# A streaming encoder layer: half sums and norm rows of the second token set inside the direct pairs, pooled products one group later

## The chip, the cores and the metric

The kernel runs on one core of a Trainium2 chip. The core's engines are TensorE (PE, with PEld for its weight loads), VectorE (DVE), ScalarE (ACT), GpSimd (POOL) and SyncE (SP), which issues the DMAs. The metric is the device time of one execution in microseconds, as a median of several; lower is better.

## The reference

One layer of a hybrid encoder works on 1024 prompt tokens and 64 sample tokens, 1088 in all, which share the weights. What is computed, cut to the core:

```python
h = rmsnorm(x); p = h @ w_in                      # split into qa, ka, va, qi, ki, wi, ub, qm, gates
a = sparse attention: per query, the top k keys by an indexer score are gathered
b = pool_mix(ub)                                  # see below
m = cross-attention of qm into 256 memory tokens
mixed = sum over the branches of sigmoid(gate) * (branch @ w_o)
x = x + mixed @ w_out
h = rmsnorm(x, g_ffn)
y = x + (silu(h @ w_gate) * (h @ w_up)) @ w_down  # D_FF = 2816

def pool_mix(u_ext):                              # 4 channel groups of 128, windows 2, 4, 8, 16
    mean_g = trailing mean of u over window_g
    p_g = mean_g - u_g
    return (p_g @ w_pool[g]) * s_pool
```

## The kernel before

All matrices are float32. Each operand is split into a rounded half `hi` and the rest `lo`, and a product is three matmuls (hi·hi, lo·hi, hi·lo). A weight block is loaded into a `raw` buffer by SP, rounded by ACT or POOL (`whi`), and its rest is taken by DVE (`wlo`, line 86).

The order of instructions on each engine is fixed when the kernel is built, by a scheduler that places them from a list of what depends on what, with gate products as fillers. An engine works through its list in order; a waiting instruction holds back all behind it.

**The pooled stage** (lines 388 to 448, in the trace from about 230 to 360 us). For each of four groups a `ub` block is multiplied (72 matmuls, into `e`), POOL doubles the window in `log2(window)` steps (`pw`, line 431), DVE forms the mean minus the token (line 435), ACT and DVE split it into `ph` and `pl` (lines 440 and 86), and three chunks of three matmuls with `pwh` and `pwl` make the pooled output, which ACT and DVE split into `bh` and `bl` (lines 446 and 447). At the same time DVE and ACT run the rounds that look for each query's k-th best score (`junk_v`, line 768; `junk_a`, line 765). PE has gate products (`fl`) as fillers, whose weights go through one buffer `fraw`. The next stage, `qm`, computes the queries of the memory attention, with weights `tmhi` and `tmlo`; the attention to memory follows at about 520 to 690 us.

**The feed-forward stage.** The tokens are two sets, 512 and 576. `w_gate` and `w_up` are walked in 11 pairs `p` of 128-row blocks. From pair 2 on, `hidden(p, (0, 1))` multiplies both sets through seven products on half sums instead of eight (`pair_product`, line 1115); seven sums of the inputs per k block (`block_sums`, lines 1061 to 1081) are needed for that. For the first set these sums are made early. For pairs 0 and 1 the first set is multiplied directly (`direct`, line 1144) while the norm rows (`norm_rows`: sums of squares line 1037, `rn` on DVE and POOL, `dg` line 1043, broadcast `ones` line 1055 into `rb`) and the sums of the second set are made; afterwards `hidden(p, (1,))` multiplies the second set for pairs 0 and 1. The sums use the tile `fr` (two buffers of 128x1024) and `ws` (four). In `pair_product` the `w_gate` blocks are loaded into `fr`, too, and the `w_up` blocks into `raw` (three buffers).

What the change touches in that stage, before:

```python
    EARLY = 2
    for p in range(EARLY):
        direct(p)
        if p == 0:
            rb = norm_rows(1, *st.pop())
        for k in (2 * p, 2 * p + 1):
            second_sums(k, rb)
```

Of the kernel before, what the change touches and what calls it, by code (L numbers as in the profile page):

```python
# [8 lines left out]
F32 = mybir.dt.float32  # L9
F32R = mybir.dt.float32r  # L10
AF = mybir.ActivationFunctionType
OP = mybir.AluOpType
# [33 lines left out]
def encoder_step(ctx: ExitStack, tc: tile.TileContext, a: dict, o: list):  # L46
# [38 lines left out]
    def lo_of(lo, src, hi):  # L85
        V.tensor_tensor(lo, src, hi.bitcast(F32), op=OP.subtract)  # L86
# [302 lines left out]
    if True:  # L389
        W0 = 15 + SEQ + 15  # L390
        E_ = W0 + DEC
        with tc.tile_pool(name="pool", bufs=1) as pp:
            fix = pp.tile([128, 4, 16], F32, name="fix")
# [9 lines left out]
            SP.dma_start(pwr.rearrange("p (g j) -> p g j", g=4), a["w_pool"])  # L403
            pwh = pp.tile([128, 4, 128], F32R, name="pwh")
            pwl = pp.tile([128, 4, 128], F32R, name="pwl")
            round_hi(pwh.rearrange("p g j -> p (g j)"), pwr)
            lo_of(pwl.rearrange("p g j -> p (g j)"), pwr, pwh.rearrange("p g j -> p (g j)"))
            for g, win in enumerate(WINDOWS):
                wts = [pp.tile([128, 1024], F32R, name=nm, tag=nm, bufs=1) for nm in ("uhi", "ulo")]
# [4 lines left out]
                for c0, cn in CH:  # L414
                    ps = mm()
                    gate_block((wh, wlo), hh[:, :, c0:c0 + cn], hl[:, :, c0:c0 + cn], ps[:, :cn])
                    m = min(cn, SEQ - c0)
                    A.copy(e[:, 15 + c0:15 + c0 + m], ps[:, :m])
                    if m < cn:
                        A.copy(e[:, W0:E_], ps[:, m:cn])  # L420
                ps = mm()
                PE.transpose(ps[:15, 0:128], e[:, SEQ:SEQ + 15], ident)
# [12 lines left out]
                V.scalar_tensor_tensor(cur[:, 31:], cur[:, 31:], 1.0 / win, e[:, 31:], op0=OP.mult, op1=OP.subtract)  # L435
                ph = pp.tile([128, T], F32R, name="ph", tag="ph", bufs=1)
                pl = pp.tile([128, T], F32R, name="pl", tag="pl", bufs=1)
                for d0, d1, s0 in ((0, SEQ, 15), (SEQ, T, W0)):
                    src = cur[:, s0:s0 + d1 - d0]
                    A.copy(ph[:, d0:d1], src)  # L440
                    lo_of(pl[:, d0:d1], src, ph[:, d0:d1])
                for c0, cn in CH:
                    c1 = c0 + cn
                    ps = mm()[:, :cn]
                    matmul3(ps, [(pwh[:, g], pwl[:, g], ph[:, c0:c1], pl[:, c0:c1])])
                    A.activation(bh[:, g, c0:c1], ps, AF.Copy, scale=spool_c[:, g:g + 1])
                    V.scalar_tensor_tensor(bl[:, g, c0:c1], ps, spool_c[:, g:g + 1], bh[:, g, c0:c1].bitcast(F32),
                                           op0=OP.mult, op1=OP.subtract)

    with tc.tile_pool(name="qm", bufs=1) as tp:  # L450
        for half in range(2):
            w = tm_weights(tp, a["w_qm"][half], 256)
            for b in range(NB):
                t0, n = TS[b]
                ps = token_major(w, b, 256)
                qn = tp.tile([128, 2, 128], F32, name="qn", tag="qn", bufs=2)
                head_norm(tp, ps, n, 2, 128, qn[:n])
                SP.dma_start(q_m[t0:t0 + n, half * 256:(half + 1) * 256], qn[:n].rearrange("p h d -> p (h d)"))


# [626 lines left out]
    def pair_product(name, p, sets, outs, finish):  # L1087
        raws = []
        for e in range(2):
            raw = fa.tile([128, 1024], F32, name="fr", tag="fr", bufs=2) if name == "w_gate" else raw_tile()  # L1090
            SP.dma_start(raw.rearrange("p (k j) -> p k j", k=KT), a[name][p + e * NP])
            raws.append(raw)
# [50 lines left out]

    def direct(p):
        n = SETS[0][1]
# [3 lines left out]
        for name in ("w_gate", "w_up"):  # L1149
            for e in range(2):  # L1150
                w = wblock(a[name][p + e * NP], (KT, 128))
                for c in range(2):
                    ps = mm()[:, :h]
                    matmul3(ps, [(w[0][:, k], w[1][:, k], blocks[c][k // 4][0][:, k % 4], blocks[c][k // 4][1][:, k % 4])
                                 for k in range(KT)])
                    t = g[:, e, c * h:c * h + h]
                    if name == "w_gate":
                        A.activation(t, ps, AF.Silu)
                    else:
                        V.tensor_tensor(t, ps, t, op=OP.mult)  # L1160
                if name == "w_up":
                    SP.dma_start(u_d[p][e, :, :n], g[:, e])

    def hidden(p, sets):
# [23 lines left out]
        pair_product("w_up", p, sets, v, up_last)  # L1188

    turn2, pair_w = [0], []  # L1190
    u_d = [dram.tile([2, 128, T], F32, name=f"u{p}") for p in range(NP)]
# [30 lines left out]

    EARLY = 2
    for p in range(EARLY):
        direct(p)
        if p == 0:
            rb = norm_rows(1, *st.pop())
        for k in (2 * p, 2 * p + 1):
            second_sums(k, rb)
    fu_c.__exit__(None, None, None)  # L1230
# [105 lines left out]
```

## Time and profile before

| | |
|---|---|
| median of three runs | 1779.03 us (1777.31 to 1780.24) |
| the profiled execution | 1782.27 us |
| its span | 1780.5 us |
| mean granted PE clock | 0.991 |
| PE busy | 1721.8 us (97%), 11810 instructions |
| DVE busy | 1127.0 us (63%) |
| ACT busy | 816.4 us (46%) |
| POOL busy | 403.3 us (23%) |
| pair products (line 1115), their share of the chain that ended last | 24% |

The profile is of one execution, a few microseconds longer than the median; the 1.8 us between span and execution lie outside what the trace records. "Busy" counts an engine's instructions; a share over the whole span is a mean over stages with different limits, so the stages that the change touches are read by themselves. A timeline row reads: start us, duration us, engine, line, operation, output <- inputs, shapes, count, and in brackets how long the engine was idle before it and what released it.

### The profile page before, as it was taken

To read this page: it belongs to the slowest core of one execution; us is meant where nothing else is said; L and a number is where in the kernel's file an instruction comes from. 1 tells how busy PE (TensorE), PEld (TensorE's weight loads), DVE (VectorE), ACT (ScalarE), POOL (GpSimd) and SP (SyncE) were. 2 spreads that over 40 slices of the span, in tenths; PEclk is the share of its full clock that TensorE was granted. 3 is DMA by queue.
4 is the path that set the end of the run, shared out by engine and by line. 5 is a ranking of instruction groups with operands and counts; after the bars stand their busy time and mean duration, and the time that the engine had idled before them with its cause. 6 is when DMAs were issued, how large, how long until landed. Compare 5 with 4: busy or idle time off the path is not lost.

```text
span 1780.5 us, 31511 instructions
## 1 busy us (share of the span) xinstructions
PE 1721.8 (97%) x11810; PEld 1672.4 (94%) x11810; DVE 1127.0 (63%) x2411; ACT 816.4 (46%) x1927; POOL 403.3 (23%) x444
## 2 busy tenths in 40 slices
PE   7999999999999998989899998999999999999999
PEld 6999999989999998877798997999999999999999
DVE  6567999998953345779783858645444444544443
ACT  5456677726523443579631444433333333433332
POOL 4111423343531223765203521100000000000000
PEclk9999999999999999999999998999999999999999
DMA  7122541134355236640454333222222221857562
GB/s 230 60 67 76 164 141 57 58 98 137 118 157 176 84 97 233 188 154 1 165 184 146 98 120 110 92 73 73 73 73 77 92 75 38 316 184 239 187 229 98
DMA packets 128582, 224.26 MB, mean 126 GB/s; under 512 B 23463, under 2 KB 86303, under 8 KB 128430
## 3 DMA queue, kind: packets, MB, share of 16 engines
q1 hardware_dynamic: 128430, 222.26, 38.5%
q8 instruction: 93, 1.52, 0.3%
q14 instruction: 59, 0.48, 0.1%
HBM read 167.84 MB, written 54.37 MB: 125 GB/s over the span
## 4 chain that ended last, share of the span: by engine, by line
PE 61%; DVE 6%; DMA 2%; issue 1%; POOL 1%; ACT 1%; SPq 0%; DVEq 0%; ACTq 0%; POOLq 0%
PE mm L1115 24%; PE mm L1263 14%; PE mm L120 11%; PE fl L120 7%; PE acc L921 1%; PE tr L891 1%; DVE lo L86 1%; PE mm L914 1%; DVE wlo L86 1%; DVE fr L1071 1%; DMA side_a<-gt 1%; DVE ws L1078 0%; PE mm L603 0%; DVE pr L895 0%; DVE pl L86 0%
## 5 line engine op out<-in xcount | busy, mean ns | idle before, releaser
L1115 PE MATMUL mm<-hi,whi 128*128 128x288 f32 (+1 forms) x1120 | 324.0, 289 | 9.4 <-ACT whi L1107 8.3
L1115 PE MATMUL mm<-hi,wlo 128*128 128x288 f32 (+1 forms) x1120 | 324.9, 291 | 0.0
L1115 PE MATMUL mm<-lo,whi 128*128 128x288 f32 (+1 forms) x1120 | 324.2, 290 | 0.0
L1115 PEld LDWEIGHTS mm<-hi,whi 128*128 128x128 f32 x1120 | 212.6, 190 | 10.1 <-ACT whi L1107 8.5
L1115 PEld LDWEIGHTS mm<-lo,whi 128*128 128x128 f32 x1120 | 212.5, 190 | 0.0
L1115 PEld LDWEIGHTS mm<-hi,wlo 128*128 128x128 f32 x1120 | 211.9, 189 | 0.2 <-DVE wlo L86 0.2
L120 PE MATMUL fl<-hl,whi 128*128 128x362 f32 (+1 forms) x576 | 190.5, 331 | 0.0
L120 PE MATMUL fl<-hh,whi 128*128 128x362 f32 (+1 forms) x576 | 189.9, 330 | 0.6 <-ACT hh L133 0.6
L120 PE MATMUL fl<-hh,wlo 128*128 128x362 f32 (+1 forms) x576 | 189.3, 329 | 0.0
L1263 PE MATMUL mm<-uh,wh 128*128 128x362 f32 (+1 forms) x512 | 167.4, 328 | 0.0
L1263 PE MATMUL mm<-ul,wh 128*128 128x362 f32 (+1 forms) x512 | 166.8, 326 | 0.0
L1263 PE MATMUL mm<-uh,wl 128*128 128x362 f32 (+1 forms) x512 | 166.0, 326 | 0.0
L86 DVE TENSOR_TENSOR wl<-raw,wh 128x1024 fp32r<-128x1024 f32 x64 | 78.4, 1225 | 126.1 <-ACT wh L94 125.8
L94 ACT CAST wh<-raw 128x1024 fp32r<-128x1024 f32 x64 | 67.3, 1051 | 148.9 <-PE mm L1263 137.5
L120 PE MATMUL mm<-tmhi,hh 128*128 128x256 f32 (+3 forms) x432 | 122.8, 289 | 0.5 <-POOL tmhi L96 0.5
L120 PE MATMUL mm<-tmlo,hh 128*128 128x256 f32 (+3 forms) x432 | 122.5, 286 | 0.3 <-DVE tmlo L86 0.3
L120 PE MATMUL mm<-tmhi,hl 128*128 128x256 f32 (+3 forms) x432 | 122.3, 285 | 0.0
L765 ACT ACTIVATE junk_a<-score,cand_a,sgn_a 128x512 f16<-128x512 f32 (+2 forms) x93 | 95.5, 1027 | 46.8 <-DVE cand_a L782 22.7
L86 DVE TENSOR_TENSOR wlo<-raw,whi 128x1024 fp32r<-128x1024 f32 (+1 forms) x75 | 76.1, 1027 | 55.0 <-ACT whi L1107 39.7
L120 PEld LDWEIGHTS fl<-hh,whi 128*128 128x128 f32 x576 | 108.3, 188 | 1.6 <-issue 1.0
L120 PEld LDWEIGHTS fl<-hl,whi 128*128 128x128 f32 x576 | 108.4, 188 | 0.6
L120 PEld LDWEIGHTS fl<-hh,wlo 128*128 128x128 f32 x576 | 108.5, 188 | 0.6
(386 smaller groups left out, 4538.5 us busy)
## 6 DMA issues: line engine op xcount, KB each, us to landing
raw<-in_w_down_dram SPq DMA_DIRECT2D x66, 512.0 KB, 3.7
raw<-in_w_up_dram SPq DMA_DIRECT2D x26, 512.0 KB, 3.7
fraw<-in_w_gates_dram SPq DMA_DIRECT2D x24, 512.0 KB, 4.0
fr<-in_w_gate_dram SPq DMA_DIRECT2D x22, 512.0 KB, 3.6
side<-side_a SPq DMA_DIRECT2D x8, 1088.0 KB, 6.0
raw<-in_w_out_dram SPq DMA_DIRECT2D x16, 512.0 KB, 3.7
uf<-u SPq DMA_DIRECT2D x44, 181.0 KB, 3.7
u<-tg SPq DMA_DIRECT2D x22, 288.0 KB, 2.1
```

What stands on the lines that cost most here:

```text
L86: V.tensor_tensor(lo, src, hi.bitcast(F32), op=OP.subtract)
L94: A.copy(hi, src)
L120: PE.matmul(ps, l, r, start=i == 0, stop=i == n - 1)
L765: A.activation(junk[:n, :nk], sc, AF.Sign, bias=bj, scale=1.0 if scale is None else scale[:n, j:j + 1], accum_out=sj)
L891: PE.matmul(lg[:n, i * 512:i * 512 + cn], qT[:, h, :n], kT[:, kv, s, k0 + c:k0 + c + cn], start=s == 0, stop=s == 1)
L914: PE.transpose(pt[:cn, i * n:(i + 1) * n], probs[i][:, c:c + cn], ident[:n, :n])
L921: PE.matmul(acc, vv, r, start=ji == 0 and i == 0, stop=ji == nj - 1 and i == 1)
L1071: V.scalar_tensor_tensor(hb[e][:, :n], ys[i][:, kk], gffn_c[:, kk:kk + 1], rb[:, :n], op0=OP.mult, op1=OP.mult)
L1115: PE.matmul(dst[i], l, r, start=start and j == 0, stop=stop and j == 11, skip_group_check=True)
L1263: PE.matmul(acc[f], l, r, start=kb == 0 and j == 0, stop=kb == NF - 1 and j == 2)
```

## The change

- In the pooled stage, the three chunks of products of a group (now `pooled`) are issued after the `ub` block of the next group; those of the last group in the `qm` stage, ahead of its fifth token block. `ph`, `pl`, `pwh` and `pwl` lie in a pool of their own (`phl`), which lives until the end of `qm`.
- `direct` takes a table `between` of what to do ahead of a weight block. The second set's norm rows are issued ahead of the second `w_gate` block of pair 0, its sums ahead of the two `w_up` blocks of pair 0 and the two `w_gate` blocks of pair 1.
- In `pair_product` the `w_gate` blocks of pairs 0 and 1 go to `raw` and their `w_up` blocks to `fr`; from pair 2 on it is as before.

```diff
--- before.py
+++ after.py
@@ -389,6 +389,10 @@
     if True:
         W0 = 15 + SEQ + 15
         E_ = W0 + DEC
+        phl_c = tc.tile_pool(name="phl", bufs=1)
+        phl = phl_c.__enter__()
+        pwh = phl.tile([128, 4, 128], F32R, name="pwh")
+        pwl = phl.tile([128, 4, 128], F32R, name="pwl")
         with tc.tile_pool(name="pool", bufs=1) as pp:
             fix = pp.tile([128, 4, 16], F32, name="fix")
             SP.dma_start(fix, bass.AP(tensor=a["fix"].tensor, offset=a["fix"].offset, ap=[[0, 128], [16, 4], [1, 16]]))
@@ -401,10 +405,18 @@
             A.copy(hc, ps[:, :64].rearrange("p (g t) -> p g t", g=4)[:, :, :15])
             pwr = raw_tile()[:, :512]
             SP.dma_start(pwr.rearrange("p (g j) -> p g j", g=4), a["w_pool"])
-            pwh = pp.tile([128, 4, 128], F32R, name="pwh")
-            pwl = pp.tile([128, 4, 128], F32R, name="pwl")
             round_hi(pwh.rearrange("p g j -> p (g j)"), pwr)
             lo_of(pwl.rearrange("p g j -> p (g j)"), pwr, pwh.rearrange("p g j -> p (g j)"))
+            def pooled(g, ph, pl):
+                for c0, cn in CH:
+                    c1 = c0 + cn
+                    ps = mm()[:, :cn]
+                    matmul3(ps, [(pwh[:, g], pwl[:, g], ph[:, c0:c1], pl[:, c0:c1])])
+                    A.activation(bh[:, g, c0:c1], ps, AF.Copy, scale=spool_c[:, g:g + 1])
+                    V.scalar_tensor_tensor(bl[:, g, c0:c1], ps, spool_c[:, g:g + 1], bh[:, g, c0:c1].bitcast(F32),
+                                           op0=OP.mult, op1=OP.subtract)
+
+            wait = []
             for g, win in enumerate(WINDOWS):
                 wts = [pp.tile([128, 1024], F32R, name=nm, tag=nm, bufs=1) for nm in ("uhi", "ulo")]
                 wh, wlo = wblock(a["w_ub"][g], (KT, 128), None, wts)
@@ -418,6 +430,8 @@
                     A.copy(e[:, 15 + c0:15 + c0 + m], ps[:, :m])
                     if m < cn:
                         A.copy(e[:, W0:E_], ps[:, m:cn])
+                if wait:
+                    pooled(*wait.pop())
                 ps = mm()
                 PE.transpose(ps[:15, 0:128], e[:, SEQ:SEQ + 15], ident)
                 PE.transpose(ps[:15, 128:256], e[:, E_ - 15:E_], ident)
@@ -433,29 +447,27 @@
                 V.tensor_tensor(cur[:, 15:31], cur[:, 15:31], fix[:, g], op=OP.mult)
                 V.tensor_tensor(cur[:, 15:31], cur[:, 15:31], e[:, 15:31], op=OP.subtract)
                 V.scalar_tensor_tensor(cur[:, 31:], cur[:, 31:], 1.0 / win, e[:, 31:], op0=OP.mult, op1=OP.subtract)
-                ph = pp.tile([128, T], F32R, name="ph", tag="ph", bufs=1)
-                pl = pp.tile([128, T], F32R, name="pl", tag="pl", bufs=1)
+                ph = phl.tile([128, T], F32R, name="ph", tag="ph", bufs=1)
+                pl = phl.tile([128, T], F32R, name="pl", tag="pl", bufs=1)
                 for d0, d1, s0 in ((0, SEQ, 15), (SEQ, T, W0)):
                     src = cur[:, s0:s0 + d1 - d0]
                     A.copy(ph[:, d0:d1], src)
                     lo_of(pl[:, d0:d1], src, ph[:, d0:d1])
-                for c0, cn in CH:
-                    c1 = c0 + cn
-                    ps = mm()[:, :cn]
-                    matmul3(ps, [(pwh[:, g], pwl[:, g], ph[:, c0:c1], pl[:, c0:c1])])
-                    A.activation(bh[:, g, c0:c1], ps, AF.Copy, scale=spool_c[:, g:g + 1])
-                    V.scalar_tensor_tensor(bl[:, g, c0:c1], ps, spool_c[:, g:g + 1], bh[:, g, c0:c1].bitcast(F32),
-                                           op0=OP.mult, op1=OP.subtract)
+                wait.append((g, ph, pl))
 
     with tc.tile_pool(name="qm", bufs=1) as tp:
         for half in range(2):
             w = tm_weights(tp, a["w_qm"][half], 256)
             for b in range(NB):
+                if half == 0 and b == 4:
+                    pooled(*wait.pop())
                 t0, n = TS[b]
                 ps = token_major(w, b, 256)
                 qn = tp.tile([128, 2, 128], F32, name="qn", tag="qn", bufs=2)
                 head_norm(tp, ps, n, 2, 128, qn[:n])
                 SP.dma_start(q_m[t0:t0 + n, half * 256:(half + 1) * 256], qn[:n].rearrange("p h d -> p (h d)"))
+
+    phl_c.__exit__(None, None, None)
 
 
     with tc.tile_pool(name="qa", bufs=1) as qp:
@@ -1087,7 +1099,7 @@
     def pair_product(name, p, sets, outs, finish):
         raws = []
         for e in range(2):
-            raw = fa.tile([128, 1024], F32, name="fr", tag="fr", bufs=2) if name == "w_gate" else raw_tile()
+            raw = raw_tile() if (name == "w_up") == (p >= EARLY) else fa.tile([128, 1024], F32, name="fr", tag="fr", bufs=2)
             SP.dma_start(raw.rearrange("p (k j) -> p k j", k=KT), a[name][p + e * NP])
             raws.append(raw)
         a11, a12 = raws[0][:, :512], raws[0][:, 512:]
@@ -1141,13 +1153,15 @@
         product(chain, a22, 3, False, True, lambda i: finish(i, t21[i], chain[i]))
 
 
-    def direct(p):
+    def direct(p, between={}):
         n = SETS[0][1]
         h = n // 2
         blocks = [[(HH[0][0][q], HH[0][1][q]) if q is not None else b12_hl for q in qs] for qs in ((0, 1), (None, 2))]
         g = fu.tile([128, 2, n], F32, name="tg", tag="tg", bufs=2)
         for name in ("w_gate", "w_up"):
             for e in range(2):
+                if (name, e) in between:
+                    between[name, e]()
                 w = wblock(a[name][p + e * NP], (KT, 128))
                 for c in range(2):
                     ps = mm()[:, :h]
@@ -1187,6 +1201,7 @@
 
         pair_product("w_up", p, sets, v, up_last)
 
+    EARLY = 2
     turn2, pair_w = [0], []
     u_d = [dram.tile([2, 128, T], F32, name=f"u{p}") for p in range(NP)]
     sq0 = out_proj(0)
@@ -1220,13 +1235,10 @@
     def second_sums(k, rb):
         block_sums(1, k, rb, HH[1], [fa.tile([128, 512], F32, name="ws", tag="ws", bufs=4) for e in range(4)])
 
-    EARLY = 2
-    for p in range(EARLY):
-        direct(p)
-        if p == 0:
-            rb = norm_rows(1, *st.pop())
-        for k in (2 * p, 2 * p + 1):
-            second_sums(k, rb)
+    rbs = []
+    direct(0, {("w_gate", 1): lambda: rbs.append(norm_rows(1, *st.pop())),
+               ("w_up", 0): lambda: second_sums(0, rbs[0]), ("w_up", 1): lambda: second_sums(1, rbs[0])})
+    direct(1, {("w_gate", 0): lambda: second_sums(2, rbs[0]), ("w_gate", 1): lambda: second_sums(3, rbs[0])})
     fu_c.__exit__(None, None, None)
     yp_c.__exit__(None, None, None)
     dn_c = tc.tile_pool(name="dn", bufs=1, side="right")
```

DVE in the first direct pair, before, from the second set's norm factors on (`rn`, `dg`; `wlo` are rests of weights of `direct`, `tg` its gated outputs, `fr<-y` the first step of a sum):

```order
L1039 TENSOR_SCALAR rn<-mm 128x5
L1043 TENSOR_SCALAR dg<-ident,rn 128x128 x5
L86 TENSOR_TENSOR wlo<-raw,whi 128x1024 x2
L1160 TENSOR_TENSOR tg<-mm,tg 128x256 x2
L86 TENSOR_TENSOR wlo<-raw,whi 128x1024
L1160 TENSOR_TENSOR tg<-mm,tg 128x256 x2
L86 TENSOR_TENSOR wlo<-raw,whi 128x1024
L1071 SCALAR_TENSOR_TENSOR fr<-y_10642,gffn_c,rb 128x576 x2
L1078 TENSOR_TENSOR ws<-fr 128x288
```

The same place after:

```order
L1051 TENSOR_SCALAR rn<-mm 128x5
L1055 TENSOR_SCALAR dg<-ident,rn 128x128 x5
L86 TENSOR_TENSOR wlo<-raw,whi 128x1024
L1083 SCALAR_TENSOR_TENSOR fr<-y_10646,gffn_c,rb 128x576 x2
L1090 TENSOR_TENSOR ws<-fr 128x288
L86 TENSOR_TENSOR lo_12280<-fr,hi_12273 128x288
L1090 TENSOR_TENSOR ws<-fr,ws 128x288
L86 TENSOR_TENSOR lo_12282<-fr,hi_12275 128x288
L86 TENSOR_TENSOR lo_12281<-fr,hi_12274 128x288
```

Before, four direct weight blocks and four outputs stood between `dg` and the first sum; now one weight block does, and sums and weight blocks alternate.

SP's queue before, from the last output of the first direct pair (`u` written from `tg`; `raw<-in_w_up` is the first pair's `w_up` for the products on half sums, `uf` a load for the last stage):

```order
L1162 DMA u_11269<-tg 128x512
L1091 DMA raw<-in_w_up_dram 128x1024 x3
L1162 DMA u_11270<-tg 128x512
L1254 DMA uf<-u_11269 128x364 x2
L1162 DMA u_11270<-tg 128x512
L1091 DMA fr<-in_w_gate_dram 128x1024 x4
L1091 DMA raw<-in_w_up_dram 128x1024 x2
L1183 DMA u_11269<-tg_12878 128x576
```

and after:

```order
L1176 DMA u_11273<-tg 128x512
L1103 DMA raw<-in_w_gate_dram 128x1024
L1266 DMA uf<-u_11273 128x364 x2
L1103 DMA fr<-in_w_up_dram 128x1024
L1103 DMA raw<-in_w_gate_dram 128x1024
L1103 DMA fr<-in_w_up_dram 128x1024
L1103 DMA raw<-in_w_gate_dram 128x1024
L1176 DMA u_11274<-tg 128x512 x2
L1103 DMA raw<-in_w_gate_dram 128x1024
```

The first two pairs' `w_gate` loads stood behind the last output of the direct stage, in `fr`; now three of them and two `w_up` loads go out ahead of these outputs, `w_gate` into `raw` and `w_up` into `fr`.

PE at the first group's pooled products (`mm<-ph,pwh`), before; `fl` is a filler, `uhi` the weights of the next `ub` block:

```order
L120 MATMUL fl<-hh,whi 128x362
L120 MATMUL fl<-hl,whi 128x362
L120 MATMUL fl<-hh,wlo 128x362
L120 MATMUL mm<-ph,pwh 128x364
L120 MATMUL mm<-ph,pwh 128x362 x2
L120 MATMUL mm<-hh,uhi 128x364
L120 MATMUL mm<-hl,uhi 128x364
L120 MATMUL mm<-hh,ulo 128x364
```

and after:

```order
L120 MATMUL mm<-hl,uhi 128x362
L120 MATMUL mm<-hh,ulo 128x362
L120 MATMUL mm<-hh,uhi 128x362
L120 MATMUL mm<-hl,uhi 128x362
L120 MATMUL mm<-hh,ulo 128x362
L120 MATMUL mm<-ph,pwh 128x364
L120 MATMUL mm<-pl,pwh 128x364
L120 MATMUL mm<-ph,pwl 128x364
L120 MATMUL mm<-ph,pwh 128x362
```

The pooled products stood behind fillers and ahead of the next `ub` block; now they stand behind that block. Between the first and the last pair of transposes of `e` (line 422 before, 436 after) PE has 506 rows before, of which 257 are fillers, and 316 after, of which 67 are fillers; DVE has 17 rounds on 64x192 before, 10 after.

## Rows read from the trace of the kernel before

**Rows 1.** Waits of PE, 1000 to 1140 us: total us, times, longest.

```profile
PE mm L1115 <- ACT whi L1107: 8.3, 1, 8.3
```

**Rows 2.** Windows: us; PE, PEld, DVE, ACT, POOL busy; PEclk; DMA share; GB/s.

```profile
1030.00:1055.00 25.00, 25.00 (x212) 25.00 (x212) 7.74 (x15) 7.10 (x11) 2.56 (x2) 1.00 0.37 116
1055.00:1077.80 22.80, 22.70 (x190) 22.50 (x188) 21.63 (x45) 12.13 (x31) 6.46 (x3) 1.00 0.28 92
1077.80:1086.00 8.20, 0.01 (x1) 0.01 (x1) 5.50 (x14) 3.59 (x9) 0.85 (x1) 0.63 0.64 205
1086.00:1109.50 23.50, 23.02 (x156) 22.56 (x156) 18.99 (x30) 11.54 (x24) 5.09 (x3) 0.91 0.28 85
```

**Rows 3.** Timeline of DVE, second half sums: start, us, operation.

```profile
1055.69 1.54 DVE L1071 SCALAR_TENSOR_TENSOR fr<-y,gffn_c,rb 128x576 f32<-128x576 f32 x2
...
1082.83 0.44 DVE L86 TENSOR_TENSOR lo<-ws,hi 128x288 fp32r<-128x288 f32 x1
```

**Rows 4.** Chain of waits, 1060 to 1140 us: start, us, what.

```profile
1079.98 5.24 DMA fr<-in_w_gate_dram
...
1085.99 23.04 PE mm L1115 x156
...
1109.57 22.62 PE mm L1115 x168
```

**Rows 5.** Waits of PE, 242 to 520 us.

```profile
PE fl L120 <- DVE fpt L549: 3.1, 2, 1.8
PE mm L120 <- ACT ph L440: 2.9, 2, 1.8
PE mm L120 <- DVE pl L86: 1.6, 1, 1.6
```

**Rows 6.** Windows, 242 to 500 us.

```profile
242.00:500.00 258.00, 251.30 (x1719) 247.76 (x1718) 239.40 (x687) 153.18 (x458) 99.55 (x108) 0.98 0.29 91
```

**Rows 7.** Timelines of PE and DVE around the second norm rows.

```profile
1034.01 0.72 PE L1037 MATMUL mm<-ones,sq 128*128 128x1 f32 x6
1034.60 0.36 PE L120 MATMUL mm<-hi,whi 128*128 128x256 f32 x1
...
1036.23 1.07 DVE L1043 TENSOR_SCALAR dg<-ident,rn 128x128 f32<-128x128 f32 x5 [1.29 <-POOL rn L1040]
1037.27 1.23 DVE L86 TENSOR_TENSOR wlo<-raw,whi 128x1024 fp32r<-128x1024 f32 x1
...
1053.39 1.22 PE L1055 MATMUL mm<-dg,ones 128*128 128x128 f32 x10
```

**Rows 8.** Timelines of DVE and ACT before the second pair ends.

```profile
1127.94 1.29 DVE L86 TENSOR_TENSOR wlo<-raw,whi 128x512 fp32r<-128x512 f32 x2 [1.25 <-ACT whi L1107]
...
1132.09 0.62 ACT L1107 CAST whi<-fr 128x512 fp32r<-128x512 f32 x1 [3.36 <-PE mm L1115]
```

**Rows 9.** Tile `fr`, 1070 to 1180 us, its loads.

```profile
DMA to landing us min/median/max: 3.6/3.7/5.2
```

**Rows 10.** Lines 435 and 422: duration ns least/median/most, first and last start.

```profile
L435 DVE SCALAR_TENSOR_TENSOR pw<-pw,e x4: 1283/1284/1285, 256.0 to 352.8; 128x1087 f32<-128x1087 f32 x4
...
L422 PE MATMUL mm<-ident,e x4: 270/272/275, 252.7 to 338.9; 128*15 128x128 f32 x4
```

**Rows 11.** Timelines of DVE and POOL, 235 to 252 us.

```profile
235.63 1.21 DVE L86 TENSOR_TENSOR ulo<-raw,uhi 128x1024 fp32r<-128x1024 f32 x1
...
242.90 0.41 DVE L768 TENSOR_SCALAR_CACHE_REDUCE junk_v<-score,cand_v 64x192 f16<-64x192 f32 x1
...
247.18 0.40 DVE L768 TENSOR_SCALAR_CACHE_REDUCE junk_v<-score,cand_v 64x192 f16<-64x192 f32 x1
...
251.66 2.84 DVE L86 TENSOR_TENSOR ulo<-raw,uhi 128x1024 fp32r<-128x1024 f32 x1
...
251.36 2.05 POOL L431 TENSOR_TENSOR pw<-e 128x1117 f32<-128x1117 f32 x1 [1.39 <-ACT e L420]
```

**Rows 12.** Timeline of PE, end of memory attention.

```profile
688.20 0.44 PE L120 MATMUL fl<-bh,whi 128*128 128x384 f32 x1 [1.40 <-DVE bl L86]
```

## The prediction

> **What bounds the kernel now.** I read four views in turn: the waits of TensorE (PE), the busy time by stretch, the chain of waits around the longest stall, and the timelines of the engines that PE waits for. PE is busy 97% of the span, so a change of order gains only where PE waits, or where it runs at the lower clock for having waited. Near the change the list of waits has one large entry: the pair products of the feed-forward part (L1115) wait once, 8.3 us, for a rounded weight, `whi` [rows 1]. By stretch [rows 2], this is the join between the two direct pairs and the first pair on half sums: PE is full until 1077.8 (22.70 of 22.80 us), does nothing until 1086, and runs at a granted clock of 0.91 in the pair after that. VectorE (DVE) shows why. It is busy 7.74 of 25 us in the first direct pair and 21.63 of 22.80 us in the second, because all of the second set's half sums are computed there: the first starts at 1055.69 and the last ends at 1083.27 [rows 3]. These sums use the two `fr` buffers, which the first `w_gate` blocks need too. So the chain [rows 4] runs through the sums to the load of `fr`, issued at 1079.98 and landed 5.24 later; behind a cast PE starts at 1085.99.
>
> The other place is the pooled stage (242 to 520 us): PE waits 3.1 for `fpt`, 2.9 for `ph` and 1.6 for `pl` there [rows 5], at a mean clock of 0.98 over 258 us with DVE busy 239 of 258 us [rows 6]. PE is kept full by gate fills (`fl`) between the pooled products.
>
> **The change part by part.** The sum is made against the profiled execution, 1782.27 us, which lies 3.24 above the median of 1779.03.
>
> *1. Sums inside the direct pairs, first gate weights through `raw`.* In the new order the sums start behind the `dg` rows of the first pair instead of at 1055.69, 18 us earlier by the trace (`dg` ends at 1037.30 [rows 7]). DVE has 25 − 7.74 = 17.3 us free in the first pair's stretch [rows 2]. The sums of the old second stretch spill 1083.27 − 1077.8 = 5.5 us past it; the room is three times that, so they end about 10 us before the direct pairs do. The first `w_gate` block now takes a `raw` buffer that the direct weights leave, and is issued before the last direct products. The wait disappears: **−8.3**. What is late next is the second `w_gate` block. SP issues it behind two `uf` loads and one `fr` load; the first product on a sum needs it one product after the first, 23.04/7 = 3.3 us later [rows 4]. I see it land 3 to 5 us ahead.
>
> *2. The clock behind the stall.* The first pair on half sums was busy 23.04 us where the next was 22.62 [rows 4]: **−0.4**. The clock of 0.91 over 23.5 us would allow 2.1 [rows 2]; since the pair's own length shows 0.4, I take that, and 2.1 as the bound.
>
> *3. Norm rows inside the first pair.* Before, 19 us lay between the sums of squares (1034.01) and the broadcast through `dg` (1053.39) [rows 7], so nothing waited. In the new order PE has 12 products in between. At 22.70/190 = 0.12 us each [rows 2] they end at 1034.60 + 1.44 = 1036.04, while DVE's last `dg` ends at 1036.23 + 1.07 = 1037.30 behind a power on GpSimd (POOL). PE waits **+1.3**. Everything on PE is queued behind it. Bounds: 0, if the sums of squares finish earlier because two of the five are now done ahead, and 2.6 if the weight block in front of `dg` on DVE delays it by its own duration (1.23 [rows 7]).
>
> *4. Pair 1 to pair 2.* `w_up` of pair 1 now sits in `fr`, and `w_gate` of pair 2 wants the same two buffers, where `raw` and `fr` alternated before. The last reader of the first block's second half is a split that ends, as the first of two, at 1127.94 + 0.65 = 1128.59 [rows 8]. A load to `fr` lands 3.6, 3.7 or 5.2 us after issue (least, median, most) [rows 9], the cast takes 0.62: PE could start at 1128.59 + 3.7 + 0.62 = 1132.91. Before, the cast stood at 1132.09, so PE started at 1132.71. **+0.3** with hops of 0.1; bounds 0.1 and 1.8 (landing 5.2). The landing decides. The Trainium skill ("DMA: Bandwidth & Descriptors", "Issuing engines are not separate DMA queues") says that all transfers interleave on the same 16 engines, and this load now meets stores of `u` and loads of `w_up`; by it the 5.2 would be the one to take and the sum would be 1.5 worse. The rows show the median nearer to the least, with the same neighbours, so I keep 0.3.
>
> *5. Pooled products one group later.* Nothing is computed that was not before; the pooled products, 9 per group, move behind the next group's `ub` block, and the last into the `qm` stage. Their waits for `ph` and `pl`, 4.5 us [rows 5], lose their direct cause, since a whole `ub` block of PE work now lies between. But the scheduler also draws the four groups together. PE's transposes ran from 252.7 to 338.9 and DVE's pooled combination from 256.0 to 352.8 [rows 10]: 86.2 and 96.8 us. Counted in the two orders, PE has 506 rows between first and last transpose before and 316 now, of which fills 257 and 67; at 86.2/506 = 0.170 each that is 53.8 us. DVE loses 7 selection rounds of 4.28 us (242.90 to 247.18) and 3 splits of 1.21 [rows 11], which makes 96.8 − 30.0 − 3.6 = 63.2. DVE falls behind PE by 10.6 before and by 9.4 now. Before, 257 fills stood there to cover it; now 67, worth 67 × 0.170 = 11.4 us, just enough. Gain of waits and loss of cover are of one size, so **0**. Bounds: −12.8 (all of [rows 5]'s 7.6 and the clock's 0.02 × 258 = 5.2 [rows 6]) and +14.3 (below, third rival).
>
> *6. Fills kept for later.* About 160 gate fills now stand at the end of memory attention, where 11 stood, and the last values finish earlier. PE's wait of 1.40 for `bl` at 688.20 [rows 12] should go: **−1.0**, bounds −1.4 and 0, as its filler could be late itself.
>
> Sum: −8.3 − 0.4 + 1.3 + 0.3 + 0 − 1.0 = −8.1, so 1774.2 in a profiled execution and **1771** as a median.
>
> **The rivals.**
>
> *The pooled stage gains too.* The waits of 4.5 us lose their cause and those for `fpt` could go with them; against it, DVE stays as busy as it was. With half to all of the 12.8: 1758 to 1765 (−8.1 − 6.4 and −8.1 − 12.8 from 1779).
>
> *The direct wait comes back in part.* For it: SP issues in order, and the second `w_gate` block stands behind `uf` and `fr` loads. If it is issued no earlier than the old first one (1079.98) it lands at the same 1085.22, and PE, which has one product of 3.3 us to do, waits 5.0: the sum is −3.1, with part 4 at its bound −1.6, so 1776 to 1777.5. Against it: its buffer is free once the direct weights are split, some microseconds earlier.
>
> *DVE sets the pooled stage, and it is slower than before.* A split next to a pooling step on POOL (2.05 us at 251.36) took 2.84 instead of 1.21 us [rows 11], 1.63 more. There are 1 + 2 + 3 + 4 = 10 such steps, and they now lie closer together. If each meets one DVE instruction of that kind, DVE is 16.3 later; of 9.4 + 16.3 = 25.7 the fills cover 11.4, so PE waits up to 14.3. With −8.1 that is 1785 as a median; with half the meetings, 1777. It decides once DVE's lateness passes the 11.4 us of fills by more than the 8.1 gained elsewhere, 19.5. For it: DVE busy 93% [rows 6] and a quarter of the fills. Against it: before, the steps met such instructions as well, so part of the 16.3 is in the 96.8 already. The Trainium skill ("SBUF — State Buffer", "Who interferes with whom") states that a DVE instruction with two SBUF inputs and a POOL instruction that reads SBUF shut each other out for a whole instruction. The split of 2.84 agrees; by the rule each meeting could cost up to the 2.05 of the step, 20.5 in all, and the time would be 1789.
>
> *Less than it says.* Should the scheduler's new order leave the sums where DVE is late anyhow, 1779 would stand; the order shows them moved, so I give this no share of its own.
>
> **How the numbers follow.** A median of this kernel can tell about 0.2%, 3.6 us, from no change: faster is below 1775.5, slower above 1782.6. Forecast 0.50 (1766 to 1775.5, from part 2 and 5's small gains to parts 3 and 4 at their bounds); pooled stage gains 0.15; direct wait comes back 0.15, of which 0.04 is faster and 0.11 the same; DVE sets the pooled stage 0.20, of which 0.07 same and 0.13 slower. Of the forecast 0.02 is the same. Faster 0.48 + 0.15 + 0.04 = 0.67, same 0.20, slower 0.13. The range 1760 to 1781 leaves out about 0.05 below and 0.14 above; the likeliest case alone has 1766 to 1775.5.
>
> **What would show it.** Part 1: no entry of several microseconds for `whi` at the pair products, the last half sum's `lo` ended before the last direct product, and a `raw` load of `w_gate` issued before it. Part 2: the first two pairs of equal length at a clock of 1.00. Part 3: a wait of 1 to 2 us at the broadcast through `dg`. Part 4: a wait under 1 us for `whi` at pair 2. Part 5: about the same PE idle time between 242 and 520 us, fewer waits for `ph` and more for `fpt` or `e`; a DVE with splits of 2.8 us throughout speaks for the third rival. Part 6: no wait for `bl` near the end of memory attention. The forecast fails if the pooled stage's idle time changes by over 4 us either way, or the attention stages behind it end later than before in spite of an equal start.

## The result and the profile after

The changed kernel took 1768.4 us (median of six runs, 1767.25 to 1774.77) against 1779.63 us for the kernel before (six runs). The ratio is 0.9944 with a 95% interval of 0.9927 to 0.9961; a second set of runs on another occasion gave 0.9935 (0.9916 to 0.9954). That is 10 to 12 us faster; 1771 was forecast, and 1768.4 lies inside the range of 1760 to 1781.

The profiled execution took 1774.77 us and was the slowest of the six, 6.4 above their median. It shows where the direct join went, but not the whole difference: 1782.27 − 1774.77 = 7.5, where the medians differ by 11.2. The section on the reasons comes back to that.

Waits of PE from 1000 to 1140 us, as in [rows 1]: line, releaser, total us, times, longest.

```profile
PE mm L120 <- DVE wlo L86: 2.2, 2, 1.1
PE mm L1127 <- DVE tu L1141: 1.1, 2, 0.6
PE mm L1049 <- POOL sq L1041: 0.6, 1, 0.6
PE mm L1067 <- DVE dg L1055: 0.3, 1, 0.3
```

The entry of 8.3 us for `whi` is gone; the new wait at the broadcast through `dg` is 0.3. Busy time by stretch, as in [rows 2]: the two direct pairs and the first two pairs on half sums, where they now lie (the stall between them has no place any more):

```profile
1031.40:1056.40 25.00, 24.70 (x207) 24.50 (x207) 19.47 (x40) 12.80 (x28) 7.80 (x5) 1.00 0.30 94
1056.40:1079.40 23.00, 23.00 (x194) 23.00 (x194) 19.41 (x37) 9.98 (x22) 6.08 (x3) 1.00 0.53 174
1079.40:1102.50 23.10, 22.55 (x169) 22.23 (x168) 16.05 (x28) 11.29 (x23) 3.35 (x2) 1.00 0.34 116
1102.50:1125.70 23.20, 22.65 (x171) 22.41 (x170) 14.03 (x25) 10.67 (x22) 1.67 (x1) 1.00 0.37 116
```

PE is full but for at most 0.55 us in each of the four, and the clock is 1.00. DVE is busy 19.47 of 25 and 19.41 of 23 us in the two direct pairs, where it had 7.74 and 21.63. The timeline of DVE answers to [rows 3, 7]:

```profile
1037.62 1.07 DVE L1055 TENSOR_SCALAR dg<-ident,rn 128x128 f32<-128x128 f32 x5 [1.29 <-POOL rn L1052]
...
1039.89 1.55 DVE L1083 SCALAR_TENSOR_TENSOR fr<-y,gffn_c,rb 128x576 f32<-128x576 f32 x2
...
1071.09 0.45 DVE L86 TENSOR_TENSOR lo<-ws,hi 128x288 fp32r<-128x288 f32 x1
1072.16 0.69 DVE L1110 TENSOR_TENSOR ws<-raw 128x512 f32<-128x512 f32 x1 [0.62 <-DMA raw<-in_w_gate_dram]
```

The sums start at 1039.89 and the last half sum ends at 1071.54; before, 1055.69 and 1083.27. The row at 1072.16 is the first to read the second `w_gate` block, directly when it landed. PE, in the same places as [rows 4, 7]:

```profile
1037.97 1.33 PE L1067 MATMUL mm<-dg,ones 128*128 128x128 f32 x10 [0.30 <-DVE dg L1055]
```
```profile
1079.38 0.28 PE L120 MATMUL mm<-hi,wlo 128*128 128x256 f32 x1
1079.50 0.30 PE L1127 MATMUL mm<-hi,whi 128*128 128x288 f32 x1
...
1081.09 0.30 PE L1127 MATMUL mm<-hi,whi 128*128 128x288 f32 x1
```

The first pair product (1079.50) follows the last direct product (1079.38) at once, and the second product, which needs the second `w_gate` block, starts at 1081.09. The chain of waits, from 1100 to 1135 us, has the row that answers to the one at 1109.57:

```profile
1101.08 22.62 PE mm L1127 x168
```

From the first pair product it stands 1101.08 − 1079.50 = 21.58 us off, before 23.58 [rows 4]. The waits of PE from 242 to 520 us, as in [rows 5]:

```profile
PE fl L120 <- DVE fpt L561: 3.5, 2, 1.9
PE mm L120 <- POOL tmhi L96: 2.0, 1, 2.0
PE mm L120 <- DVE tmlo L86: 1.5, 2, 1.2
PE mm L120 <- ACT ph L454: 0.4, 1, 0.4
PE mm L120 <- DVE ulo L86: 0.3, 1, 0.3
```

The waits for `ph` and `pl`, 4.5 us, have become 0.4; in their place stand 2.0 for `tmhi` and 1.5 for `tmlo`, the weights of `qm`. The lines of the pooled stage, as in [rows 10], and after them two that mark the feed-forward part (sums of squares, pair products): durations in ns, first and last start.

```profile
L449 DVE SCALAR_TENSOR_TENSOR pw<-pw,e x4: 1285/1286/1286, 256.2 to 320.2; 128x1087 f32<-128x1087 f32 x4
```
```profile
L436 PE MATMUL mm<-ident,e x4: 270/272/275, 252.7 to 306.2; 128*15 128x128 f32 x4
```
```profile
L1049 PE MATMUL mm<-ones,sq x18: 165/250/271, 980.4 to 1035.9; 128*128 128x1 f32 x18
```
```profile
L1127 PE MATMUL mm<-hi,whi x1120: 280/288/404, 1079.5 to 1507.6; 128*128 128x288 f32 x103, 128*128 128x256 f32 x84
```

The same two marks before:

```profile
L1037 PE MATMUL mm<-ones,sq x18: 165/250/271, 979.0 to 1034.5; 128*128 128x1 f32 x18
```
```profile
L1115 PE MATMUL mm<-hi,whi x1120: 274/288/610, 1086.0 to 1515.4; 128*128 128x288 f32 x104, 128*128 128x256 f32 x83
```

From these marks every run below can be cut into stretches that depend little on what happened earlier: from the last sum of squares to the first pair product (1079.5 − 1035.9 = 43.6 us after the change, 1086.0 − 1034.5 = 51.5 before), and from the first pair product to the last (1507.6 − 1079.5 = 428.1, before 1515.4 − 1086.0 = 429.4).

### The profile page after: what moved, and what is told of

Read it like the earlier page. It is cut to its first block, busy times and chain, and to the rows that moved or that the text cites. A ratio compares the mean times of both kernels' runs of the same rounds, so it can differ in the third digit from the quotient of the medians.

```text
span 1772.7 us, 31533 instructions
## 1 busy us (share of the span) xinstructions
PE 1719.6 (97%) x11810; PEld 1668.6 (94%) x11810; DVE 1124.5 (63%) x2411; ACT 813.6 (46%) x1927; POOL 409.5 (23%) x444
## 4 chain that ended last, share of the span: by engine, by line
PE 76%; DVE 11%; ACT 3%; issue 3%; DMA 3%; POOL 2%; SPq 0%; DVEq 0%; ACTq 0%; POOLq 0%
PE mm L1127 24%; PE mm L120 17%; PE mm L1275 15%; PE fl L120 13%; DVE junk_v L780 2%; ACT junk_a L777 2%; PE acc L933 1%; PE tr L903 1%; PE mm L333 1%; DVE wlo L86 1%; PE mm L926 1%; DMA gt<-side_m 1%; DVE lo L86 1%; DVE pl L86 1%; DVE tmlo L86 1%
```

## The experiments

Theory 1 was that the join behind the direct pairs gives the whole gain; theory 2, that the pooled stage gives some of it. The two halves of the change don't touch each other's order of PE, so they can be run apart. The ratios below are worked out from all runs and can differ a little from those of the medians.

### Both halves, each half alone, and the sums without the buffers

The whole change again:

> The changed kernel once more, on the same chip as its parts. Theory 1 (the join behind the direct pairs gives the whole gain, the pooled stage nothing): 8 to 11 us under the kernel before. Theory 2 (the pooled stage gives some 3 us of it, which the one profile hides behind a low clock): the same number; only the parts tell the two apart.

1767.08 us, ratio 0.9935.

Only the pooled part:

```diff
+            wait = []
             for g, win in enumerate(WINDOWS):
...
+                if wait:
+                    pooled(*wait.pop())
...
-                ph = pp.tile([128, T], F32R, name="ph", tag="ph", bufs=1)
+                ph = phl.tile([128, T], F32R, name="ph", tag="ph", bufs=1)
```

> Only the pooled products one group later; the direct pairs as before. Theory 1: 0 us, within 1.5 of the kernel before, since the attention behind it starts a little earlier and then waits for other things. Theory 2: 3 us faster, and the attention ends earlier by as much. The rival of the prediction (DVE sets the pooled stage): slower by up to 10.

1776.16 us against 1778.54, ratio 0.9987 (0.9976 to 0.9998): 2.3 us faster, barely clear of nothing. The third rival, a slower pooled stage, falls.

Only the direct part:

```diff
+    direct(0, {("w_gate", 1): lambda: rbs.append(norm_rows(1, *st.pop())),
+               ("w_up", 0): lambda: second_sums(0, rbs[0]), ("w_up", 1): lambda: second_sums(1, rbs[0])})
...
+            raw = raw_tile() if (name == "w_up") == (p >= EARLY) else fa.tile([128, 1024], F32, name="fr", tag="fr", bufs=2)
```

> Only the norm rows and half sums inside the direct pairs and the first gate weights in the other buffers; the pooled stage as before. Theory 1: the whole gain, 8 to 11 us. Theory 2: 7 to 8.5, the wait of 8.3 and the clock behind it less the wait at the broadcast.

1768.25 us, ratio 0.9951 (0.9935 to 0.9966), 8.7 us; the medians differ by 10.3. With the 2.3 of the pooled part 8.7 makes the 11 of both, as theory 2 has it, but it lies in the 8 to 11 of theory 1 and not in the 7 to 8.5 of theory 2. So the join gives most of the gain, and these two runs don't tell the theories apart.

The same without the exchanged buffers:

```diff
-            raw = raw_tile() if (name == "w_up") == (p >= EARLY) else fa.tile([128, 1024], F32, name="fr", tag="fr", bufs=2)
+            raw = fa.tile([128, 1024], F32, name="fr", tag="fr", bufs=2) if name == "w_gate" else raw_tile()
```

> The sums and norm rows inside the direct pairs, but the gate weights in their old buffers, which the sums use too. If the early sums are what counts, the buffers are free near 1070 us, the load lands before the direct products end, and 7 to 11 us are gained as with both. If the other buffers are needed, because SP's queue or the sums still hold the loads back, a wait of 3 to 6 us for the first gate weight stays and 2 to 5 are gained.

1767.08 us, ratio 0.9944 (0.9924 to 0.9964): not to be told from the time with them. The buffers aren't needed once the sums are early.

### Which edit of the direct part does it

Only the buffers (that is, the line above the other way round, in the kernel before):

> Only the gate weights of pairs 0 and 1 in the other buffers; norm rows and sums behind the direct pairs as before, the pooled stage as before. If the wait of 8.3 us was one for the weight's load alone, it goes and 8 are gained. Theory: the load is the last of two causes; the sums of the second set still end about 5.5 us behind the direct products, the first product needs their first parts near 1079 us, and waits of 1 to 4 us stay: 4 to 7 gained.

1777.18 us, ratio 0.9997 (0.9983 to 1.0011): nothing. It did less than the theory's 4 to 7. The chain of waits of this kernel from 1060 to 1095 us (start, us, what) tells why:

```profile
1075.26 3.04 DMA u<-tg
...
1078.47 0.40 ACT tg L1131
1078.87 0.33 ACT hi L1079
1079.20 0.53 ACT whi L1107
...
1079.78 15.27 PE mm L1115 x92
```

and its mark lines:

```profile
L1037 PE MATMUL mm<-ones,sq x18: 165/250/271, 974.2 to 1029.7; 128*128 128x1 f32 x18
```
```profile
L1115 PE MATMUL mm<-hi,whi x1120: 276/288/606, 1072.7 to 1508.9; 128*128 128x288 f32 x103, 128*128 128x256 f32 x84
```

The load is early and the first pair product starts 43.0 us after the last sum of squares. But then PE waits 5.3 us inside the first pair: ACT's `whi` stands behind a `tg` copy, which waits for the store of the direct pairs' output (`u`), and behind a cast (`hi`) of the late sums. The pair products take 1508.9 − 1072.7 = 436.2 us, 429.4 before (1086.0 to 1515.4). From the last sum of squares to the last pair product it is 479.2 us; before it was 480.9 (1034.5 to 1515.4). The wait moved behind the first products and became little shorter.

Only the norm rows:

```diff
+    direct(0, {("w_gate", 1): lambda: rbs.append(norm_rows(1, *st.pop()))})
+    for k in (0, 1):
+        second_sums(k, rbs[0])
+    direct(1)
+    for k in (2, 3):
+        second_sums(k, rbs[0])
```

> The norm rows inside the first direct pair, nothing else: sums written behind the direct pairs, weights in their old buffers, pooled stage as before. Theory: the order already puts the sums on VectorE as soon as the norm rows are there, so this alone gives all of the direct part, 8 to 11 us, as with the sums between. Rival: the sums have to be written between the blocks, and most of the 8.3 stays.

1767.55 us, ratio 0.9940 (0.9920 to 0.9959): everything the direct part gives. DVE's first and last rows of the half sums, and the mark lines:

```profile
1035.23 1.55 DVE L1071 SCALAR_TENSOR_TENSOR fr<-y,gffn_c,rb 128x576 f32<-128x576 f32 x2
...
1066.42 0.45 DVE L86 TENSOR_TENSOR lo<-ws,hi 128x288 fp32r<-128x288 f32 x1
```
```profile
L1037 PE MATMUL mm<-ones,sq x18: 165/250/271, 975.7 to 1031.2; 128*128 128x1 f32 x18
```
```profile
L1115 PE MATMUL mm<-hi,whi x1120: 274/288/399, 1074.8 to 1502.8; 128*128 128x288 f32 x104, 128*128 128x256 f32 x83
```

The sums run from 1035.23 to 1066.87 although they are written behind the pairs; the scheduler had only waited for the norm rows. 43.6 and 428.0 us, as in the changed kernel.

### The pooled part

The whole change without the exchanged buffers:

> The whole change but for the exchanged buffers. Theory: the buffers give nothing once the sums are early, so the time is that of the whole change, 1767 to 1768; without the load that meets its own buffer at the third pair it could be 0.1 to 0.3 better, which can't be told. Rival: the buffers matter in the join with the pooled change as well, 1770 or more.

1766.26 us, ratio 0.9936 (0.9916 to 0.9955): as the whole change.

Only a pool of its own for `ph`, `pl`, `pwh` and `pwl`, the products in their old place:

```diff
+        phl_c = tc.tile_pool(name="phl", bufs=1)
+        phl = phl_c.__enter__()
...
-                ph = pp.tile([128, T], F32R, name="ph", tag="ph", bufs=1)
+                ph = phl.tile([128, T], F32R, name="ph", tag="ph", bufs=1)
```

> Only a pool of their own for the pooled products' operands, with the products where they were; direct pairs as before. Theory: the 2.4 us of the pooled part come from the products' later place, so this gives 0 within 1.5. Rival: the gain comes from the qm weights no longer sharing memory with the pooled operands, and is found here, 2 to 3 us.

1782.26 us, ratio 1.0029 (1.0016 to 1.0041): 5 us slower, 3.3 by the medians, which neither theory had. So the later place of the products gives some 6 to 7 us against this pool. To see whether the pool of its own costs that in the new place as well, the products one group later with the old pool, the last group's right behind its own:

```diff
-                ph = phl.tile([128, T], F32R, name="ph", tag="ph", bufs=1)
+                ph = pp.tile([128, T], F32R, name="ph", tag="ph", bufs=1)
                 wait.append((g, ph, pl))
+            pooled(*wait.pop())
...
-                if half == 0 and b == 4:
-                    pooled(*wait.pop())
```

> Pooled products one group later, but with their operands in the stage's own pool as before, and the last group's products right behind the last group; direct pairs as before. Theory: the pool of its own costs 3 us by itself and the later products give 5 to 7, so this is 4 to 6 us faster than the kernel before. Rival: the later place of the last group's products, inside qm, is what carries the gain, and this is no faster than the kernel before, or slower.

1775.87 us against 1776.87, ratio 0.9984 (0.9969 to 1.0000). That is 1 us by the medians and 2.8 by the ratio, not the 4 to 6 of the theory, and no clear gain; the rival, no gain without the later place inside `qm`, isn't excluded. With norm rows and sums in front:

> The same pooled stage with the norm rows and sums inside the direct pairs, buffers as before. Theory: 1763 to 1765, below the whole change. Rival: 1768 or more.

1765.81 us, ratio 0.9929 (0.9907 to 0.9950): between the 1763 to 1765 of the theory and the 1768 of the rival, the lowest of all, but not to be told from the whole change (0.9935) or from it without the buffers (0.9936).

## Why the prediction was right

**Parts 1 and 3, the wait and the norm rows.** From the last sum of squares to the first pair product the time fell from 51.5 us to 43.6, 7.9 us, and to 43.6 in each of the seven profiled executions that have the norm rows early. Forecast were −8.3 + 1.3 = −7.0. The wait went as told. The term that was mis-sized is part 3: 0.3 instead of 1.3. I let PE wait for the last of the five `dg` (1037.30). The row of after has the first broadcast matmul at 1037.97, 0.35 after the first `dg` began (1037.62) and before the last ended (1038.69). What was late next also came earlier than told: the second `w_gate` block was there at 1072.16, 8.9 us before the product that needs it (1081.09), not 3 to 5. The 3.3 us that I gave to one product were wrong: the piece of 23.04 us has 156 matmuls [rows 4], and a product on half sums of one set has 12 (four k blocks, three matmuls each), so that these are 13 products and one takes 1.6 us at full clock (1081.09 − 1079.50). The second rival, priced with 3.3, was 1.7 too cheap. The sums ended 8.0 us before the first pair product (1071.54), where I had told about 10.

What the prediction had wrong in part 1 is which edit carries it. It gave the sums and the buffers one part in the removal each. The runs show that the norm rows' place alone does it, that the buffers alone only move the wait, and that the two together are no more than the first.

**Parts 2 and 4, clock and third pair.** From the first to the last pair product it was 429.4 us before and is 428.1 now, −1.3, where −0.4 + 0.3 was told. Both terms were too small in this profile. The stretch behind the stall, 23.58 us before, is 21.58 now at a clock of 1.00: −2.0, which is the bound that the clock of 0.91 gave (2.1) and not the 0.4 that I took; I had compared the busy times of two pieces of the chain as if they were alike, but the first has 156 matmuls and the second 168 [rows 4], so it should have been shorter by more than a microsecond, and was longer. The whole loss lies directly behind the stall. The same stretch before, in two windows:

```profile
1085.99:1090.01 4.02, 4.02 (x15) 3.80 (x16) 3.99 (x5) 1.54 (x3) 1.73 (x1) 0.50 0.00 0
1090.01:1109.57 19.56, 19.01 (x142) 18.77 (x142) 15.05 (x27) 10.07 (x21) 3.36 (x2) 1.00 0.34 103
```

The first 15 matmuls took 4.02 us at a granted clock of 0.50. The first 15 of the changed kernel take 1.99 (1079.50 to 1081.49), and what follows up to the row of 22.62 us is as long as before (19.59 and 19.56).

The exchange of the buffers costs 0.7 at the third pair (pair 2), not 0.3. ACT's copy out of a product of pair 2, before and in the changed kernel:

```profile
1143.68 0.40 ACT L1135 COPY tg<-mm 128x288 f32<-128x288 f32 x1 [1.22 <-PE mm L1115]
```
```profile
1135.88 0.40 ACT L1147 COPY tg<-mm 128x288 f32<-128x288 f32 x1 [1.22 <-PE mm L1127]
```

From the row of 22.62 us (1109.57 before, 1101.08 now) it stands 34.11 us off before and 34.80 now. The 0.3 was also worked out from the wrong row: I let PE begin the third pair at 1132.71, behind the cast at 1132.09. PE's first product of that pair, the first on the set of 512 tokens, before and now:

```profile
1134.43 0.27 PE L1115 MATMUL mm<-hi,whi 128*128 128x256 f32 x1
```
```profile
1126.04 0.39 PE L1127 MATMUL mm<-hi,whi 128*128 128x256 f32 x1
```

Before, it started at 1134.43, 1.7 us later than I took it, right behind the last matmul of the second pair (1134.30). So a load that lands in 3.7 us, with its cast done at 1132.91, would have cost nothing. The loads landed later. Into `fr`, 1105 to 1135 us of the changed kernel:

```profile
DMA to landing us min/median/max: 3.6/5.1/5.8
```

Of these three the two of the third pair, issued together at 1120.2 and 1120.8, took 5.1 and 5.8 us; before, issued at 1116.6 and 1119.3, they took 3.6 each. This fits what the Trainium skill says ("DMA: Bandwidth & Descriptors", "Issuing engines are not separate DMA queues"): transfers run on the same 16 engines and interleave. I had kept the smaller figure.

Over the whole stretch the exchange costs less, because without it PE waits in the first pair for a copy out of its own product. From the kernel with the norm rows alone:

```profile
1078.64 0.40 PE L1115 MATMUL mm<-hi,whi 128*128 128x288 f32 x1 [0.45 <-ACT tg L1131]
...
1131.14 0.40 ACT L1135 COPY tg<-mm 128x288 f32<-128x288 f32 x1 [1.22 <-PE mm L1115]
```

From the first pair product to the copy in pair 2 it is 56.1 to 56.9 us in the three profiled executions with the exchange and early norm rows, and 56.0 to 56.3 in the four that have early norm rows without the exchange: 0.3 more in the mean, inside the spread. That this is the figure of the forecast is chance.

So −7.9 − 2.0 + 0.7 = −9.2 for the join, −7.1 as told. With the 2.3 of the pooled part, which was told as −1.0, it makes −11.5 where the medians show −11.2 and −8.1 was told: the `dg` wait, the clock and the pooled part all erred to the same side, and the range held them.

**Part 5, the pooled stage.** DVE's combinations now span 320.2 − 256.2 = 64.0 us and PE's transposes 53.5; told were 63.2 and 53.8. PE was not held up by this: its waits between 242 and 520 us are 8.6 before (the 7.6 of [rows 5] and 1.0 in smaller ones) and 7.7 after: `ph` and `pl` gave back 4.1, `fpt`, `tmhi` and `tmlo` took 3.1 (the two last had 0.8 before). That a split on DVE and a step on POOL hold each other up, as in [rows 11], did not decide the time: DVE's span came out 0.8 us longer than told, and the third rival's 14.3 us are not there. **Part 6:** the wait of 1.4 for `bl` became one of 0.8 for `gt`, −0.6 instead of −1.0.

**What the pooled part's 2.3 us are.** Not the stage itself: from the first transpose of `e` to the first score product of the attention, the profiled kernels with the old pooled order and pool took 446.2, 443.2, 445.6, 442.6 and 443.2 us, those with both new 444.2, 442.5, 442.4 and 443.0, 1.1 less in the mean with a spread of 2 to 4. (With the products later and the old pool it was 438.7 and 439.7, and the whole was hardly faster for it.) From there to the last sum of squares it was 336.1 and 333.2 in the mean, again within the spread. This part of the attention varies with the clock from one execution to the next, for the same kernel. Two executions of the changed kernel show it. PE at the start of the attention (`tr` are scores, `fl` a filler that waits for a gate row) in the profile of the result:

```profile
696.88 0.97 PE L903 MATMUL tr<-kT,qT 128*128 128x384 f32 x4 [1.10 <-ACT qT L884]
699.15 0.69 PE L120 MATMUL fl<-bh,whi 128*128 128x384 f32 x1 [1.31 <-DVE gt L580]
...
706.96 1.65 PE L903 MATMUL tr<-kT,qT 128*128 128x384 f32 x4 [0.66 <-DVE mx L907]
```

and in that of the repetition:

```profile
695.00 0.97 PE L903 MATMUL tr<-kT,qT 128*128 128x384 f32 x4 [1.10 <-ACT qT L884]
696.35 0.45 PE L120 MATMUL fl<-bh,whi 128*128 128x384 f32 x1 [0.38 <-DVE gt L580]
...
701.80 1.09 PE L903 MATMUL tr<-kT,qT 128*128 128x384 f32 x4 [1.00 <-DVE mx L907]
```

and by windows, 700 to 710 us, of the first and of the second (the third figure from the end is the clock):

```profile
700.00:705.00 5.00, 4.34 (x14) 3.83 (x13) 1.14 (x7) 1.07 (x3) 1.61 (x2) 0.50 1.00 342
705.00:710.00 5.00, 4.34 (x13) 3.83 (x13) 3.77 (x12) 2.90 (x11) 2.27 (x3) 0.50 1.04 366
```
```profile
700.00:705.00 5.00, 4.00 (x20) 3.09 (x20) 3.74 (x12) 3.62 (x12) 2.42 (x3) 1.00 1.05 380
705.00:710.00 5.00, 4.80 (x37) 4.52 (x35) 3.37 (x8) 3.51 (x8) 4.28 (x6) 1.00 0.87 312
```

In the first, PE waited 1.31 us for `gt` and the clock fell; the same score products took 1.65 us instead of 1.09, and from 1.9 us at the first row (696.88 to 695.00) the two are 5.2 apart at the third (706.96 to 701.80). In the second the wait was 0.38 and the clock stayed at 1.00. From the first score product to the last sum of squares the two executions differ by 6.1 us (339.0 and 332.9), which is most of the 7.5 between their spans (1772.7 and 1765.2). Five of the six executions of the changed kernel had a mean clock of 0.996 or more, the profiled one 0.993; so its profile shows only 7.5 us of the 11.2.

The prediction called it a sign of failure if the attention ended later in spite of an equal start. In the profile of the result it did: its first score product came 2.0 us earlier than before (696.9 and 698.9), and the last sum of squares behind it 1.4 later (1035.9 and 1034.5). In the repetition that came 6.6 earlier (1027.9). A single profile can't carry this sign.

**What stays open.** Why a pool of its own with the products in their old place costs 5 us: its one profile (1778.6 us of span, faster than its median) has the same lengths of stages as before, so nothing in it shows the loss. And whether the pooled part's 2.3 us come from fewer waits at the start of the attention or from chance: its interval ends at 0.9998, and with the norm rows early it adds nothing that can be told (0.9940 without it, 0.9936 with it, on one occasion). The profiles lean to the first. In all six with the products in their old place a filler behind the first score product waits 1.08 to 3.03 us for `gt`, and within 10 us the clock falls. With the later products that wait is 1.31 in the profile of the result, 0.38 in the repetition and absent in the other four, and in four of these six the clock stays at 1.00 for the first 20 us. That is one execution of each kernel, and no run changes that wait alone.

## What to carry to other kernels

Before an early load or another buffer is made for a stall, ask what feeds the work that holds the buffer: here a broadcast of five columns, one call placed three weight blocks later than needed, held back 27.6 us of sums (1055.69 to 1083.27), and moving that call alone gave the whole gain of the join. Here the stall had two causes in a row, and removing the later one alone gave nothing (0.9997); it only changed which instruction waits. Cut the profile into stretches between marks on the same engine: one of these lengths agreed to 0.1 us in seven executions, where 20 whole times of the kernel before ran from 1772.45 to 1783.84.

## What the runs showed of the hardware

At the start of the attention the granted clock goes with several microseconds, and waits that differ little stand beside either level. In two executions of the same kernel, the windows of 700 to 705 and 705 to 710 us stand at 0.50, the lower of the two levels (1.2 GHz), after waits of 1.10 and 1.31 us, and at 1.00 (2.4 GHz) after 1.10 and 0.38. The 0.93 us more of waiting came with 3.3 us more by the third row (5.16 − 1.88). The two waits alone don't settle it: in the kernel with the exchanged buffers alone PE waited 1.10 and 1.08 us at this place, and the clock stood at 1.00 for another 5.4 us (697.37 to 702.80) and at 0.59 in the 2.5 us after that.

Behind the stall of 8.3 us before the change, the granted clock was 0.50 for 4.02 us of work and 1.00 after it: 15 matmuls took 2.0 us more than at full clock.
